# The first 512 columns of q and of k in one pass over x: both weight streams interleaved at the start of a decoder block

## The chip, the cores and the metric

The kernel runs on one core of one Trainium2 chip. The metric is the device time of one execution in microseconds (us), median of several runs.

## What is computed

A decoder block for one sequence of 256 tokens with a model width of 2048, in float32:

```python
hn   = rms_norm(h, pre_mix_norm)
proj = hn @ w_in                      # 2048 -> 1024 (pool) + 1024 (q) + 1024 (k) + 1024 (v)
pool = causal_multiscale_pool(u_pool, pool_w, pool_scale)
q, k = apply_partial_rope(q, positions), apply_partial_rope(k, positions)
attn = differential_attention(q, k, v, lam)          # 8 heads, causal, 256 x 256
h    = h + rms_norm(concat([pool, rms_norm(attn)]) @ w_out, post_mix_norm)
hn   = rms_norm(h, pre_ffn_norm)
h    = h + rms_norm((silu(hn @ w_gate) * (hn @ w_up)) @ w_down, post_ffn_norm)   # 5632 wide
```

The change concerns the very first products: `hn @ w_in` for the first 512 columns of q and the first 512 columns of k.

## The kernel before

**Products.** Every float32 product is made of three TensorE (PE) matmuls in a reduced float type: the operands are split into a high part (a rounded copy, made by ScalarE, ACT) and a low part (the rest, made by VectorE, DVE), and high x high, low x high and high x low are added up in PSUM. `mm_a` (lines 132 to 137) issues these three for one of the 16 slices of 128 rows of the contraction (a "k" of x below) and one of two blocks `t` of 128 tokens; 512 columns of weights stream through each matmul. So one k of x with 512 columns takes 2 x 3 = 6 matmuls, and 512 columns of output over all 16 k take 96.

**Weights.** They come from HBM in pieces of 128 partitions x 1024 elements (512 KB), that is two k of 512 columns, into a ring of `RAW = 6` raw tiles. `ring_parts` gives the split tiles: a ring of `RING = 3` pairs (`whi`, `wlo`). A raw tile is free for the next load when both halves of its split are done; a split tile is free when the last matmul on it is done. All loads but two are issued by SyncE's queue (SP), in the order of the program.

**The first product.** The first 512 columns of q are computed by a loop written out by hand (lines 269 to 293), because x itself arrives at the same time. Each x slice comes transposed (`xT`), is scaled by the norm's gain and split by `x_in` (lines 253 to 255: one ACT and one DVE instruction per k). For the first four k, weights and x come in single-k pieces (256 KB and 128 KB); from then on x comes four k at a time (512 KB) and weights in 512 KB pieces. The two results accumulate in the PSUM banks `ps0`.

**What follows.** After this loop stand the loads of positions, of constants and of x itself once more (2 MB, for the norm's statistics: `load_after` holds them behind the latest weight load), the squares and sums of x (line 308, ACT), the reciprocal root, and the sines and cosines. Then a loop over two groups `g` of four heads computes q, k and v with 512 columns each: `gemm_a` with the weights' ring, then `heads_in` (scale by the norm's factor `rq` or `r1`, rotate, transpose on PE), then the heads' attention (`head`), whose scores use the PSUM tile `sc` (two banks), the pooling branch and `heads_out`. For `g == 0`, q is what the first loop left in `ps0`, and k is a `gemm_a` of its own (line 514).

**Order.** Each engine executes its own instructions in a fixed order. That order is chosen when the program is built: a scheduler runs a simulated timeline and may put a later instruction ahead of an earlier one of the same engine, save where a dependence or `issue_after` forbids it. On the chip an engine then waits at whatever instruction stands next.

Of the kernel before, what the change touches and what calls it, by code (L numbers as in the profile page):

```python
# [8 lines left out]
F32 = mybir.dt.float32  # L9
F32R = mybir.dt.float32r  # L10
I32 = mybir.dt.int32
AF = mybir.ActivationFunctionType
ALU = mybir.AluOpType
AX = mybir.AxisListType

P = 128
S = 256
D = 2048
NKD = D // P
# [26 lines left out]
def block_kernel(ctx: ExitStack, tc: tile.TileContext, x, xT, pos, cols, rows, lamv, invf, invcnt,  # L46
                 w_in, w_u, w_pool, w_out, w_g0, w_u0, w_gu, w_down, out):
    nc = tc.nc
    mm, act, dve, pool, sync = nc.tensor, nc.scalar, nc.vector, nc.gpsimd, nc.sync
# [10 lines left out]
    def nm(s):  # L60
        uid[0] += 1
        return f"{s}_{uid[0]}"
# [4 lines left out]
    def bank():  # L67
        return psum.tile([P, 512], F32, tag="mm", name=nm("mm"), bufs=4)

    def bank2():  # L70
        return psum.tile([P, 512], F32, tag="tr", name=nm("tr"), bufs=2)


    latest = [None]

    def raw_tile(half=0):
        return ring.tile([P, 1024], F32, tag="raw", name=nm("raw"), bufs=RAW)
# [3 lines left out]
    def load(src, half):  # L81
        raw = raw_of[0](half)
        latest[0] = sync.dma_start(raw, src[:, half * 1024:(half + 1) * 1024]).ins
        return raw
# [6 lines left out]
    def ring_parts():  # L91
        return (ring.tile([P, 1024], F32R, tag=f"w{z}", name=nm(f"w{z}"), bufs=RING) for z in ("hi", "lo"))
# [18 lines left out]
    def a_steps(srcs, order=None, held=range(0), parts=None):  # L111

        i = 0
        for s in order or range(len(srcs)):
            raws = [load(srcs[s], half) for half in range(2)]
            for half in range(2):
                by = parts(i) if i in held else ()
                if by != "halves":
                    hi, lo = split(raws[half], *by)
                for j in range(2):  # L120
                    c = slice(j * 512, (j + 1) * 512)
                    if by == "halves":
                        w = split(raws[half][:, c], lambda: (half_tile("wh"), half_tile("wl")))
                    else:
                        w = hi[:, c], lo[:, c]
                    yield i, 4 * s + 2 * half + j, *w
                    i += 1
# [4 lines left out]
    def mm_a(ps, a, t, k, wh, wl, first, last):  # L132

        with tc.issue_after(behind[0]) if behind[0] is not None else nullcontext():
            mm.matmul(ps[t][:, :], lhsT=a[0](k, t), rhs=wh, start=first, stop=False)  # L135
            mm.matmul(ps[t][:, :], lhsT=a[1](k, t), rhs=wh, start=False, stop=False)  # L136
            last_mm[0] = mm.matmul(ps[t][:, :], lhsT=a[0](k, t), rhs=wl, start=False, stop=last).ins  # L137
# [3 lines left out]
    def gemm_a(srcs, a, nk, order=None, before=lambda i: None):  # L141
        ps = [bank(), bank()]
        for i, k, wh, wl in a_steps(srcs, order):
            before(i)
            for t in range(2):
                mm_a(ps, a, t, k, wh, wl, i == 0, i == nk - 1)
        return ps
# [85 lines left out]
    psum_sc = p_att.enter_context(tc.tile_pool(name="psum_sc", bufs=1, space=bass.MemoryType.PSUM))  # L233
    ap_ = p_att.enter_context(tc.tile_pool(name="ap", bufs=1))
# [16 lines left out]
    vtag = lambda name: ap_.tile([P, 1024], F32, tag="v", name=nm(name), bufs=2)  # L251

    def x_in(k, xr):
        act.activation(xh_k(k), xr, AF.Copy, scale=g1(k))
        dve.scalar_tensor_tensor(xl_k(k), xr, g1(k), xh_k(k).bitcast(F32), ALU.mult, ALU.subtract)
# [10 lines left out]
    a_x = (lambda k, t: xh_k(k)[:, t * P:(t + 1) * P], lambda k, t: xl_k(k)[:, t * P:(t + 1) * P])  # L266


    ps0 = [bank(), bank()]
    for i in range(4):  # L270
        xr = ap_.tile([P, 4, S], F32, tag="qk", name=nm("xr"), bufs=2) if i < 2 else vtag("xr").rearrange("p (a b) -> p a b", b=S)
        if i > 0:
            sync.dma_start(xr, xT[:, 4 * i:4 * i + 4, :])
        raws = [load(w_in[0, i], half) if i > 0 else raw_tile() for half in range(2)]
        for half in range(2):
            hi, lo = ring_parts()
            raw = raws[half]
            if i > 0:
                act.activation(hi, raw, AF.Copy)  # L279
            for j in range(2):  # L280
                k = 4 * i + 2 * half + j
                c = slice(j * 512, (j + 1) * 512)
                if i == 0:
                    (act if k == 0 else sync).dma_start(xr[:, k:k + 1, :], xT[:, k:k + 1, :])
                    latest[0] = sync.dma_start(raw[:, c], w_in[0, 0][:, half * 1024 + j * 512:half * 1024 + (j + 1) * 512]).ins
                x_in(k, xr[:, k - 4 * i, :])
                if i == 0:
                    act.activation(hi[:, c], raw[:, c], AF.Copy)
                if i == 0 or j == 0:
                    d = c if i == 0 else slice(0, 1024)  # L290
                    dve.tensor_tensor(lo[:, d], raw[:, d], hi[:, d].bitcast(F32), ALU.subtract)
                for t in range(2):
                    mm_a(ps0, a_x, t, k, hi[:, c], lo[:, c], k == 0, k == NKD - 1)


    post_t = tiny.tile([P, 2], I32, tag="pos", name="post", bufs=1)
# [67 lines left out]
    def heads_in(ps, scale, what, g):  # L364
        n = ap_.tile([P, 2, 512], F32, tag="qk", name=nm(what), bufs=2)
        for t in range(2):
            act.activation(n[:, t, :], ps[t][:, :], AF.Copy, scale=scale[:, t:t + 1])
        v = n.rearrange("p t (h d) -> p t h d", d=64)
        r16 = v[:, :, :, 0:16]
        shape = [P, 2, 8, 16]  # L370
        ra = ap_.tile(shape, F32, tag="ra", name=nm("ra"), bufs=1)
        rb = ap_.tile(shape, F32, tag="rb", name=nm("rb"), bufs=1)
        for t in range(2):
            cb = cos2[:, t].rearrange("p a b -> p (a b)")[:, None, :].to_broadcast([P, 8, 16])
            sb = sin2[:, t].rearrange("p a b -> p (a b)")[:, None, :].to_broadcast([P, 8, 16])
            dve.tensor_tensor(ra[:, t], r16[:, t], cb, ALU.mult)
            dve.tensor_tensor(rb[:, t], r16[:, t], sb, ALU.mult)
        dve.tensor_tensor(v[:, :, :, 0:8], ra[:, :, :, 0:8], rb[:, :, :, 8:16], ALU.subtract)
        dve.tensor_tensor(v[:, :, :, 8:16], ra[:, :, :, 8:16], rb[:, :, :, 0:8], ALU.add)
        res = []  # L380
        for hp in range(2):
            tr = bank2()
            for j in range(2):
                for t in range(2):
                    mm.transpose(tr[:, j * S + t * P: j * S + (t + 1) * P], n[:, t, (2 * hp + j) * P:(2 * hp + j + 1) * P], ident)
            o = mid.tile([P, 2, S], F32, tag="qkT", name=nm(what + "T"), bufs=8)
            act.activation(o.rearrange("p a b -> p (a b)"), tr[:, :], AF.Copy)
            res.append(o)
        return res
# [121 lines left out]
    for g in range(2):  # L511
        ps = ps0 if g == 0 else gemm_a([w_in[3 * g, i] for i in range(4)], a_x, NKD)
        qT += heads_in(ps, rq, "q", g)
        ps = gemm_a([w_in[3 * g + 1, i] for i in range(4)], a_x, NKD)
        kT += heads_in(ps, r1, "k", g)
        if g == 1:
            pool_mix(1)
        ps = gemm_a([w_in[3 * g + 2, i] for i in range(4)], a_x, NKD)
        for t in range(2):
            act.activation(vt[t][:, g * 512:(g + 1) * 512], ps[t][:, :], AF.Copy, scale=r1[:, t:t + 1])  # L520
        for h in range(4 * g, 4 * g + 4):
            head(h)
        for i in (3 - 2 * g, 2 - 2 * g):
            pool_u(i)
        heads_out(g)
# [132 lines left out]
    ps = gemm_a([w_u0[i] for i in range(4)], a_h, NKD, None, lambda i: h_sums(h_at[i]) if i in h_at else None)  # L658
# [84 lines left out]
    for c in range(1, NF // 4):  # L743
        m = {1: bank(), 2: bank(), 3: bank(), 4: bank(), 5: None, 6: bank2(), 7: psum_m.tile([P, 512], F32, tag="m7", name=nm("m7"), bufs=1), 8: bank2()}
# [165 lines left out]
```

## Time and profile before

| | |
|---|---|
| median of 3 runs | 1042.12 us (1040.69 to 1042.84) |
| the profiled execution | 1042.59 us, of which the profile's span is 1040.8 us |
| granted TensorE clock, mean | 0.997 |
| PE busy | 1018.6 us (98% of the span), 4787 matmuls |
| DVE busy | 733.4 us (70%) |
| ACT busy | 538.8 us (52%) |
| HBM read | 198.37 MB, 195 GB/s over the span |

A row of the profile's timeline reads: start, duration (both in us, from the span's start), engine, source line, operation, output<-inputs, shapes, count of merged instructions; in brackets, how long the engine sat idle before it and what ended that. `SPq` and `ACTq` are the instruction queues of SyncE and ScalarE that issue transfers. `PEld` is the load of a matmul's stationary operand. A matmul's row shows a duration of some 0.39 us, but matmuls overlap: the pitch is the distance from one start to the next.

### The profile page before, as it was taken

Reading aid. Unit: us, or ns where it says so; the run is one execution under the profiler, and the core shown is the slowest. Engines: PE = TensorE matmul, PEld = TensorE weight load, DVE = VectorE, ACT = ScalarE, POOL = GpSimd, SP = SyncE. Lnnn points to the kernel's source line nnn. Section 1 sums busy time; section 2 is a strip of 40 time slices with the busy share of each in tenths; the row PEclk is TensorE's granted clock in tenths of the full one; section 3 lists DMA queues with packets and bytes.
Section 4 is the critical chain, followed back from the end, with each engine's and each line's share of the span. In section 5 each row is a group of like instructions: output and inputs, shape, how many; then the busy total and the mean of one; then the engine's idle time right before and its main releaser. Section 6 shows DMA issues by size and latency. Waiting matters only on the chain.

```text
span 1040.8 us, 12565 instructions
## 1 busy us (share of the span) xinstructions
PE 1018.6 (98%) x4787; PEld 839.4 (81%) x4787; DVE 733.4 (70%) x847; ACT 538.8 (52%) x643; POOL 34.6 (3%) x57
## 2 busy tenths in 40 slices
PE   8999999999999999999999999999999999999996
PEld 5788888988877788888878878878888888888884
DVE  6648755875677978889798887888877664454444
ACT  6746545664547655454554545545555653343431
POOL 0003200210030000000000000000000000000000
PEclk9999999999999999999999999999999999999998
DMA  8853555456754556555655556645565575556542
GB/s 321 293 182 122 178 185 166 156 168 220 245 198 158 175 207 207 180 181 207 212 191 186 177 191 211 209 167 183 199 211 202 206 286 193 194 192 212 195 169 81
DMA packets 57517, 203.39 MB, mean 195 GB/s; under 512 B 6896, under 2 KB 7792, under 8 KB 56688
## 3 DMA queue, kind: packets, MB, share of 16 engines
q1 hardware_dynamic: 57168, 202.44, 56.8%
q8 instruction: 37, 0.61, 0.2%
q14 instruction: 24, 0.20, 0.1%
q10 hardware_dynamic: 288, 0.15, 0.0%
HBM read 198.37 MB, written 4.19 MB: 195 GB/s over the span
## 4 chain that ended last, share of the span: by engine, by line
PE 85%; DMA 6%; DVE 6%; issue 1%; SPq 1%; ACT 1%; DVEq 0%; ACTq 0%
PE mm L137 15%; PE mm L136 15%; PE mm L135 15%; PE mm L757 8%; PE mm L755 7%; PE mm L756 7%; DMA raw<-in_w_gu 4%; PE tr L757 2%; PE tr L756 2%; PE tr L755 2%; DVE wl L695 2%; PE mm L173 2%; PE mm L175 2%; PE mm L174 1%; PE m L755 1%; DVE xn L563 1%
## 5 line engine op out<-in xcount | busy, mean ns | idle before, releaser
L100 DVE TENSOR_TENSOR wl<-raw,wh 128x1024 fp32r<-128x1024 f32 x88 | 104.7, 1222 | 106.9 <-ACT wh L99 106.9
L100 DVE TENSOR_TENSOR wlo<-raw,whi 128x1024 fp32r<-128x1024 f32 x97 | 119.2, 1230 | 70.3 <-ACT whi L99 64.0
L99 ACT ACTIVATE wh<-raw 128x1024 fp32r<-128x1024 f32 x88 | 89.3, 1052 | 122.0 <-PE mm L136 117.3
L99 ACT ACTIVATE whi<-raw 128x1024 fp32r<-128x1024 f32 x97 | 102.1, 1057 | 78.0 <-PE mm L136 60.7
L136 PE MATMUL mm<-wh,gl 128*128 128x512 f32 x352 | 137.1, 390 | 0.0
L695 DVE TENSOR_TENSOR wl<-raw,wh 128x2048 fp32r<-128x2048 f32 x50 | 114.4, 2287 | 31.2 <-ACT wh L702 31.2
L135 PE MATMUL mm<-wh,gh 128*128 128x512 f32 x352 | 134.8, 389 | 0.0
L137 PE MATMUL mm<-wl,gh 128*128 128x512 f32 x352 | 130.7, 389 | 0.0
L755 PE MATMUL mm<-wh,h 128*128 128x512 f32 x330 | 128.6, 390 | 0.0
L756 PE MATMUL mm<-wh,h 128*128 128x512 f32 x330 | 128.6, 390 | 0.0
L757 PE MATMUL mm<-wl,h 128*128 128x512 f32 x330 | 115.6, 394 | 3.8 <-DVE wl L695 3.8
L702 ACT ACTIVATE wh<-raw 128x2048 fp32r<-128x2048 f32 x50 | 95.5, 1910 | 44.7 <-PE tr L756 39.8
L702 ACT ACTIVATE wh<-T 128x2048 fp32r<-128x2048 f32 x30 | 57.3, 1911 | 60.4 <-DVE T L706 55.4
L695 DVE TENSOR_TENSOR wl<-T,wh 128x2048 fp32r<-128x2048 f32 x30 | 68.6, 2287 | 23.1 <-ACT wh L702 23.1
L135 PE MATMUL mm<-whi,x 128*128 128x512 f32 x192 | 75.1, 395 | 3.5 <-ACT whi L279 2.7
L137 PEld LDWEIGHTS mm<-wl,gh 128*128 128x128 f32 x352 | 66.1, 188 | 13.7
L136 PEld LDWEIGHTS mm<-wh,gl 128*128 128x128 f32 x352 | 66.0, 188 | 13.8
L757 PEld LDWEIGHTS mm<-wl,h 128*128 128x128 f32 x330 | 61.9, 188 | 18.7 <-DVE wl L695 6.1
L135 PEld LDWEIGHTS mm<-wh,gh 128*128 128x128 f32 x352 | 66.0, 188 | 13.5
L136 PE MATMUL mm<-whi,x 128*128 128x512 f32 x192 | 74.6, 391 | 0.0
L756 PEld LDWEIGHTS mm<-wh,h 128*128 128x128 f32 x330 | 61.9, 188 | 13.0
L755 PEld LDWEIGHTS mm<-wh,h 128*128 128x128 f32 x330 | 62.0, 188 | 12.6
(243 smaller groups left out, 1910.6 us busy)
## 6 DMA issues: line engine op xcount, KB each, us to landing
raw<-in_w_gu SPq DMA_DIRECT2D x160, 512.0 KB, 4.5
raw<-in_w_down SPq DMA_DIRECT2D x88, 512.0 KB, 4.1
raw<-in_w_in SPq DMA_DIRECT2D x46, 512.0 KB, 3.7
raw<-in_w_out SPq DMA_DIRECT2D x32, 512.0 KB, 4.0
raw<-in_w_u SPq DMA_DIRECT2D x24, 512.0 KB, 3.6
raw<-in_w_g SPq DMA_DIRECT2D x8, 512.0 KB, 5.9
xn<-in_x SPq DMA_DIRECT2D x2, 1024.0 KB, 9.1
gain<-in_rows SPq DMA_DIRECT2D x8, 256.0 KB, 4.9
```

Source lines behind the costliest of these rows:

```text
L99: last_split[0] = act.activation(hi, raw, AF.Copy).ins
L100: (by or dve).tensor_tensor(lo, raw, hi.bitcast(F32), ALU.subtract)
L135: mm.matmul(ps[t][:, :], lhsT=a[0](k, t), rhs=wh, start=first, stop=False)
L136: mm.matmul(ps[t][:, :], lhsT=a[1](k, t), rhs=wh, start=False, stop=False)
L137: last_mm[0] = mm.matmul(ps[t][:, :], lhsT=a[0](k, t), rhs=wl, start=False, stop=last).ins
L173: mm.matmul(o, lhsT=wh, rhs=xh, start=st, stop=False)
L175: mm.matmul(o, lhsT=wl, rhs=xh, start=False, stop=sp)
L695: last_low[0] = dve.tensor_tensor(res, x, hi.bitcast(F32), ALU.subtract).ins
L702: act.activation(res, x, AF.Copy)
L755: mm.matmul(o, lhsT=a[0], rhs=wh, start=first, stop=False)
L756: mm.matmul(o, lhsT=a[1], rhs=wh, start=False, stop=False)
L757: mm.matmul(o, lhsT=a[0], rhs=wl, start=False, stop=left[i] == 0)
```

## The change

The first loop now goes over the 16 k of x and, for each, does q's 512 columns and k's 512 columns one after the other: 12 matmuls for each k of x where there were 6. q accumulates in `ps0` as before, k in `ps1`, which is the first use of the PSUM tile `sc` that the heads' scores use later. Only the first two k come in single-k pieces; x of k = 2 and 3 comes as one 256 KB piece, the rest of x four k at a time; from k = 2 on weights come in 512 KB pieces, q's and k's in turn. The loads are issued in the order x, q's weights, k's weights. The `gemm_a` for k of the first group is dropped; the loads of positions and constants and of x for the statistics now stand behind the loads of both weight streams, since `latest` is then the last of them.

```diff
     ps0 = [bank(), bank()]
-    for i in range(4):
-        xr = ap_.tile([P, 4, S], F32, tag="qk", name=nm("xr"), bufs=2) if i < 2 else vtag("xr").rearrange("p (a b) -> p a b", b=S)
-        if i > 0:
-            sync.dma_start(xr, xT[:, 4 * i:4 * i + 4, :])
-        raws = [load(w_in[0, i], half) if i > 0 else raw_tile() for half in range(2)]
-        for half in range(2):
-            hi, lo = ring_parts()
-            raw = raws[half]
-            if i > 0:
-                act.activation(hi, raw, AF.Copy)
-            for j in range(2):
-                k = 4 * i + 2 * half + j
-                c = slice(j * 512, (j + 1) * 512)
-                if i == 0:
-                    (act if k == 0 else sync).dma_start(xr[:, k:k + 1, :], xT[:, k:k + 1, :])
-                    latest[0] = sync.dma_start(raw[:, c], w_in[0, 0][:, half * 1024 + j * 512:half * 1024 + (j + 1) * 512]).ins
-                x_in(k, xr[:, k - 4 * i, :])
-                if i == 0:
-                    act.activation(hi[:, c], raw[:, c], AF.Copy)
-                if i == 0 or j == 0:
-                    d = c if i == 0 else slice(0, 1024)
-                    dve.tensor_tensor(lo[:, d], raw[:, d], hi[:, d].bitcast(F32), ALU.subtract)
-                for t in range(2):
-                    mm_a(ps0, a_x, t, k, hi[:, c], lo[:, c], k == 0, k == NKD - 1)
+    sc0 = psum_sc.tile([P, 2, 512], F32, tag="sc", name="sc0", bufs=1)
+    ps1 = [sc0[:, t] for t in range(2)]
+    xrs = [ap_.tile([P, 4, S], F32, tag="qk", name=nm("xr"), bufs=2) if i < 2 else vtag("xr").rearrange("p (a b) -> p a b", b=S) for i in range(4)]
+    raws = {}
+    for k in range(NKD):
+        n = 1 if k < 2 else 2
+        i, j = k // 4, k % 4
+        if k < 2 or k % 4 == 0 or k == 2:
+            x_z = slice(j, j + (1 if k < 2 else 2 if k == 2 else 4))
+            (act if k == 0 else sync).dma_start(xrs[i][:, x_z, :], xT[:, k:k + x_z.stop - x_z.start, :])
+        if j % 2 == 0:
+            raws = [(raw_tile(), *ring_parts()) for _ in range(2)]
+        for m in range(2):
+            raw, hi, lo = raws[m]
+            c = slice(j % 2 * 512, (j % 2 + n) * 512)
+            if n == 1 or j % 2 == 0:
+                latest[0] = sync.dma_start(raw[:, c], w_in[m, i][:, j * 512:(j + n) * 512]).ins
+        x_in(k, xrs[i][:, j, :])
+        for m in range(2):
+            raw, hi, lo = raws[m]
+            if n == 1 or j % 2 == 0:
+                c = slice(j % 2 * 512, (j % 2 + n) * 512)
+                act.activation(hi[:, c], raw[:, c], AF.Copy)
+                dve.tensor_tensor(lo[:, c], raw[:, c], hi[:, c].bitcast(F32), ALU.subtract)
+            c = slice(j % 2 * 512, (j % 2 + 1) * 512)
+            for t in range(2):
+                mm_a((ps0, ps1)[m], a_x, t, k, hi[:, c], lo[:, c], k == 0, k == NKD - 1)
...
-        ps = gemm_a([w_in[3 * g + 1, i] for i in range(4)], a_x, NKD)
+        ps = ps1 if g == 0 else gemm_a([w_in[3 * g + 1, i] for i in range(4)], a_x, NKD)
         kT += heads_in(ps, r1, "k", g)
```

## The prediction

> **What bounds the kernel now.** First the page: the span's share of each engine and the chain of work that ended last.
>
> ```profile
> span 1040.8 us, 12565 instructions
> ...
> PE 1018.6 (98%) x4787; PEld 839.4 (81%) x4787; DVE 733.4 (70%) x847; ACT 538.8 (52%) x643; POOL 34.6 (3%) x57
> ...
> PE 85%; DMA 6%; DVE 6%; issue 1%; SPq 1%; ACT 1%; DVEq 0%; ACTq 0%
> ```
>
> PE is the bound, and the change neither adds nor removes a matmul. A gain can come only from PE's idle time, 1040.8 - 1018.6 = 22.2 us in all. PE's waits in the first 130 us, apart from the very start, name two:
>
> ```profile
> PE mm L135 <- ACT whi L279: 2.7, 1, 2.7
> ...
> PE mm L135 <- ACT whi L99: 0.8, 1, 0.8
> ```
>
> One lies in the rewritten stage (line 279), one at the seam behind it (line 99); PE's timeline gives places and sizes.
>
> ```profile
> 5.24 1.15 PE L135 MATMUL mm<-whi,x 128*128 128x512 f32 x2
> ...
> 7.16 0.62 PE L135 MATMUL mm<-whi,x 128*128 128x512 f32 x2
> 7.61 0.61 PE L136 MATMUL mm<-whi,x 128*128 128x512 f32 x2
> ...
> 10.78 0.61 PE L137 MATMUL mm<-wlo,x 128*128 128x512 f32 x2
> 14.11 0.50 PE L135 MATMUL mm<-whi,x 128*128 128x512 f32 x1 [2.71 <-ACT whi L279]
> ...
> 15.93 0.40 PE L135 MATMUL mm<-whi,x 128*128 128x512 f32 x1
> ...
> 30.70 0.39 PE L137 MATMUL mm<-wlo,x 128*128 128x512 f32 x1
> 31.86 0.50 PE L135 MATMUL mm<-whi,x 128*128 128x512 f32 x1 [0.77 <-ACT whi L99]
> ...
> 33.68 0.40 PE L135 MATMUL mm<-whi,x 128*128 128x512 f32 x1
> ```
>
> The undisturbed pitch is (7.61 - 7.16) / 2 = 0.227 us. The first 24 matmuls (four k of q) run from 5.24 to about 11.24; the first six need 1.92 us instead of 1.36, since the low part of x comes late. The next matmul starts at 14.11: 2.87 us lost. The six starts from 14.11 to 15.93 take 1.82 instead of 1.36 (the low part of the weights comes late): 0.46. At the seam from q to k, 30.70 to 31.86 is 0.93 too much, and 31.86 to 33.68 again 0.46: together 1.39.
>
> What ended these waits is seen on ACT and DVE, and behind them in the transfers:
>
> ```profile
> 8.24 0.63 ACT L288 ACTIVATE whi<-raw 128x512 fp32r<-128x512 f32 x1
> 11.40 1.71 ACT L254 ACTIVATE x<-xr,colt 128x256 fp32r<-128x256 f32 x4 [2.53 <-DMA xr<-in_xT]
> 13.01 2.10 ACT L279 ACTIVATE whi<-raw 128x1024 fp32r<-128x1024 f32 x2
> ...
> 26.33 1.91 ACT L308 ACTIVATE junk<-xn 128x2048 bf16<-128x2048 f32 x1 [2.54 <-DMA xn<-in_x]
> ...
> 30.76 1.04 ACT L99 ACTIVATE whi<-raw 128x1024 fp32r<-128x1024 f32 x1
> 31.82 1.28 ACT L197 ACT_TABLE_LOAD   x1
> ...
> 14.09 2.36 DVE L291 TENSOR_TENSOR wlo<-raw,whi 128x1024 fp32r<-128x1024 f32 x2 [0.46 <-ACT whi L279]
> ```
>
> At 11.40 the second piece of x lands; ACT then makes four high parts of x (1.71) and only then the first high part of weights (1.05), at whose end PE starts. At the seam, 2 MB of x for the statistics stand between q's and k's weights; ACT does their squares first and k's first split at 30.76. Both losses are transfers' arrivals:
>
> ```profile
> 5.00:10.00 5.00, 5.00 (x21) 3.96 (x20) 3.85 (x8) 3.27 (x7) 0.00 (x0) 1.00 0.94 302
> 10.00:15.00 5.00, 2.29 (x11) 1.49 (x9) 2.60 (x5) 3.60 (x6) 0.00 (x0) 1.00 1.01 396
> ```
>
> (Busy time of PE, PEld, DVE, ACT, POOL, then granted clock, DMA share, GB/s.) From 10 us on the transfers are saturated, at 396 GB/s (DMA share 1.01).
>
> **The change, part by part.**
>
> *Demand.* Before, two k of q take 256 KB of x and 512 KB of weights for 12 matmuls (2.73 us): 288 GB/s. Now one k takes 128 + 512 KB for 12 matmuls: 240 GB/s. Both are below 396; what counts is the order of arrival.
>
> *The start.* x of k = 0 is issued by ACT as before, but SP's second transfer is now k's 256 KB of weights instead of 128 KB of x, so x may land later by up to 128 KB, 0.35 us at some 380 GB/s (between the 302 and the 396 of the first two windows, nearer to the second). PE then starts between 5.24 and 5.59. I take 0.3, and it is covered: the 24 matmuls (now two k) then end at 11.5, before the next weights can be split.
>
> *The next weights (largest term).* Ahead of the first 512 KB piece there stand, before, four weight pieces of 256 KB and four x pieces of 128 KB; now four of 256 KB, two of 128 KB and one of 256 KB: 1536 KB both times. So q's weights for k = 2, 3 take the place of x's second piece, landing at 11.40. Earliest: the last small weights were split from 8.24 without a wait, and a 512 KB piece later takes 1.28 us (between x's second and fourth piece lie six such pieces, and that fourth one lands at 8.78 + 10.29 = 19.07: 7.67 / 6), so 9.5. Latest: one piece later, 12.7. I take 11.4, since the queue is filled the same way. x of k = 2 and 3 has landed by then, so ACT's split follows at once: 11.4 + 1.05 = 12.45, PE restarts at 12.5. Before it did at 14.11. Gain 1.6; the ends give 2.5 (no stall at all: 14.11 - 11.57) and 0.3.
>
> ```profile
> 8.78 10.29 DMA xr<-in_xT
> 19.09 9.74 DMA xn<-in_x
> ```
>
> *The late low part.* DVE's subtraction takes 1.18 to 1.22 and starts when ACT ends; four matmuls (0.91) stand before its first use. Same shape as at 14.11: 0.46 lost again, difference 0 (ends 0 and +0.46, should the bank order give it eight matmuls to hide in).
>
> *The weights after that.* By 1.28 us per 512 KB: k's for k = 2, 3 at 12.7, x at 14.0, the next pair at 15.2 and 16.5, where PE wants them at 12.5 + 5.46 + 0.46 = 18.4. From there transfers run ahead. Stall 0.
>
> *The seam.* The 2 MB of x now queue behind all of q's and k's weights, and what comes next on PE is v, wanted after 168 more matmuls from 12.5: 12.5 + 0.46 + 38.1 = 51. The last weight load waits for a raw tile until 30.2 (worked out below). Unhurried loads take 3.7 us to land:
>
> ```profile
> raw<-in_w_in SPq DMA_DIRECT2D x46, 512.0 KB, 3.7
> ```
>
> So that one lands at 33.9, x behind it at 36.5 and 39.0 (2.56 us per MB), then v's first weights. All are there before 51, so the 1.39 goes. Cover: 12 us of matmuls; without it the cost is again about 1.4. What is late next is no transfer: v's weights, 512 KB per 12 matmuls (2.73 us), are 192 GB/s, half of the 396.
>
> *Split tiles.* Here the change costs something. With three split tiles and two streams, the k half of a pair reuses the tile of the q half one pair earlier: free after 18 of that pair's 24 matmuls, wanted 12 matmuls (2.73 us) later, its low part 4 later still (3.64). Split takes 1.05 + 1.22, so 1.2 us of slack; before, a tile was free 24 matmuls (5.46 us) ahead. The same count gives the last load: tile of the fifth pair (12.96 + 2 x 5.46 + 4.1 is 28, split until 30.2). In that phase ACT also does two squares of 1.91 and table loads of 1.28. One of them falling into the 2.7 us at its worst costs 1.91 - 1.2 = 0.7 of PE. Ends: 0 and 2 x 0.7 + 3 x 0.1 = 1.7; I take 0, since the chance that a 1.9 us piece covers the one moment per 5.46 us with over 1.2 left is (1.9 - 1.2) / 5.46, about 1 in 8.
>
> *heads_in* for q moves from k's product to v's: both then share v's 21.8 us (96 matmuls). The rows for it:
>
> ```profile
> L367 ACT ACTIVATE k<-mm,r 128x512 f32<-128x512 f32 x2 | 1.4, 684 | 0.9 <-PE mm L137 0.9
> ...
> 52.07 1.09 ACT L387 ACTIVATE qT<-tr 128x512 f32<-128x512 f32 x2 [1.83 <-PE tr L385]
> ...
> 45.96 0.49 DVE L376 TENSOR_TENSOR ra<-q,cos 128x128 f32<-128x128 f32 x2
> 46.62 0.28 DVE L378 TENSOR_TENSOR q<-ra,rb 128x128 f32<-128x128 f32 x1
> ```
>
> ACT: 8 splits of 1.05, 4 copies of 0.68, two pairs of 1.09, 13.3 us. DVE: 8 x 1.2 and, for each of q and k, 2 x 0.49 + 2 x 0.28, 12.9 us. Both fit. PE's transposes only move. The scores' PSUM tile is wanted after v, long after k's copy out of it. Cost 0; uncovered, it would delay v's splits by a copy, 0.7.
>
> Sum: 1.6 + 0 + 1.39 = 3.0. The profiled execution took 1042.59 (span 1040.8 and 1.8 around), so 1039.6; the median of the runs lies 0.47 lower, hence **1039.1**.
>
> **The rivals.**
>
> *A faster second pair (0.17).* q's second weights land near 9.5. For: the transfer share was 0.94 in 5 to 10, not 1.0. Against: the same 1536 KB ahead. Gain 2.5 + 1.39 = 3.9, up to 4.3 with the low part hidden: 1038.2 to 1037.8.
>
> *Slack eaten (0.30): no measurable change.* ACT waits at the square for x, as it did at 26.33 (2.54), with a split queued behind. Behind x's second MB at 39.0 a square and 0.2 of read-out (to 41.1) and the split (42.2) meet a want of 40.3 (the seventh pair's q half, 12.96 + 5 x 5.46) to 41.7 (its k half): 0.5 to 1.9 lost, and the table loads take their 0.1 each. Gain 0.8 to 2.2: 1039.9 to 1041.3, taken as up to 2.1. For: slack falls from 5.46 to 2.73. Against: x now comes with little queued ahead.
>
> *Statistics too late (0.09): slower.* One mechanism: x's second half lands late, and ACT's order has both squares ahead of the splits of the seventh pair; PE's wait is then landing + 2.1 + 1.05 - 40.3. At 39.0 that is 1.9; over 42.3 it exceeds 3.0 + 2.1 and the kernel is slower by over 0.2%. At 43 it gives 1042.1 + 2.9 = 1045.0. Against: x took 9.74 from issue with a full queue; issued at 32 and lying for 9.74 again it would land at 41.8, which is not yet enough.
>
> *The clock (0.03).* PE's idle stretch before the second pair grows and PE restarts slowly. The 9 warm-up matmuls of the same shape take 4.02 / 9 = 0.45 each:
>
> ```profile
> 1.45 4.02 PE L249 MATMUL tr<-warm 128*128 128x512 bf16 x9 [1.45 <-DVE warm L245]
> ```
>
> Should a restart be as slow for as long as those (9 x 0.22 = 2.0 lost) after weights 2.5 us later than forecast, the gain is 3.0 - 4.5: 1043.6. Against: the 2.71 idle at 14.11 left the granted clock at 1.00, and the pitch behind it at 0.23. The Trainium skill, "TensorE: Matmul & The Clock Gate", Part 1 (the HAM clock gate), states that an idle window of about 3.4 us halves the clock; the trace agrees so far as 2.71 did not do it. By that rule the weights would have to land past 13.9.
>
> **How the numbers follow.** 0.2% is 2.1 us, about what a measurement here can tell from no change. Likeliest (0.41): 3.0 saved, 1039.1, own range 1038.5 to 1040.0. With the faster second pair (0.17) that is 0.58 faster. Slack eaten (0.30) and the clock (0.03) are within 0.2%: 0.33. Slower 0.09. The range runs from 1037.4 (4.3 gained, and 0.4 for the spread of the runs) to 1042.4; the slower case and the edge of the clock's lie outside.
>
> **What would show it.** Right: PE's second restart at 12 to 13 us with 24 matmuls before it, waiting for ACT's `whi` and this for a weight transfer, not x; no gap of PE between 18 and 51; squares of x on ACT between 35 and 41. Wrong: PE waiting on `whi` or `wlo` between 30 and 51, ACT idle for `xn` just ahead of a split, or the matmuls that turn `r1` into a row (line 214) waiting on DVE.

## The result and the profile after

The changed kernel takes 1058.24 us (1053.71 to 1062.06, 4 runs), the one before in the same runs 1042.44: ratio 1.0154, interval 1.0132 to 1.0175. It is slower by 1.5%, where 1039.1 was forecast. The profiled execution took 1060.05 us. Its page begins:

```profile
span 1058.2 us, 12574 instructions
...
PE 1022.4 (97%) x4787; PEld 840.4 (79%) x4787; DVE 732.7 (69%) x847; ACT 538.3 (51%) x643; POOL 36.4 (3%) x57
...
PE 77%; DVE 9%; DMA 7%; issue 4%; ACT 2%; SPq 0%; DVEq 0%; ACTq 0%
```

The work is the same (4787 matmuls, 847 and 643 instructions on DVE and ACT), the span is 17.4 us longer, and in the chain PE's share fell from 85% to 77%: PE waits for others more often. The next view is PE's waits, of the first 130 us (first fence) and of the whole kernel (second).

```profile
PE mm L135 <- ACT x L254: 0.9, 1, 0.9
PE mm L135 <- ACT whi L292: 0.3, 1, 0.3
```

```profile
PE mm L760 <- DVE wl L698: 5.6, 8, 1.3
PE mm L758 <- ACT rh L705: 5.5, 6, 1.6
PE m L758 <- ACT gT L679: 5.0, 9, 0.7
PE mm L758 <- ACT wh L705: 3.9, 4, 1.0
```

Where the change was made, the waits of 2.7 and 0.8 us are gone. The new ones, 20.0 us against 4.3 (`PE mm L757 <- DVE wl L695: 3.8, 4, 1.2` and 0.5 for `rh`), stand in the FFN's loop over ten chunks of gate and up weights, whose code the change does not touch (its lines are 3 higher after). To see when the time goes, take the start of the n-th matmul in both traces (counted from 0, the 9 warm-ups included; up to each number in the table the same kinds of matmuls have been done, as often) and subtract:

| matmul | where | before | after | difference |
|---|---|---|---|---|
| 33 | second pair of the first stage | 14.11 | 12.45 | -1.66 |
| 129 | behind the seam | 37.80 | 34.70 | -3.10 |
| 716 | behind the first four heads | 141.74 | 136.85 | -4.89 |
| 1770 | ahead of the FFN loop | 346.44 | 342.02 | -4.42 |
| 4200 | behind it | 897.27 | 914.69 | +17.42 |
| 4786 | the last | 1030.10 | 1047.52 | +17.42 |

The start gained 4.9 us, more than forecast, and the FFN loop lost 21.8. Of these, 15.7 are PE's listed waits (20.0 - 4.3) and some 3.4 are two stretches of 3.41 us at half clock in the loop (last section); the other 2.7 are not attributed. The windows show in what form the time is lost (busy us of PE, PEld, DVE, ACT, POOL; clock; DMA share; GB/s), one chunk of the loop in each: one of before, then four of after:

```profile
401.00:444.00 43.00, 42.97 (x193) 34.93 (x192) 36.48 (x31) 23.41 (x19) 0.00 (x0) 1.00 0.56 194
```

```profile
401.00:450.00 49.00, 44.73 (x197) 35.36 (x195) 38.79 (x33) 23.69 (x19) 0.00 (x0) 1.00 0.49 172
450.00:492.00 42.00, 41.50 (x185) 34.36 (x186) 33.95 (x29) 22.00 (x16) 0.00 (x0) 1.00 0.58 201
492.00:542.00 50.00, 46.49 (x199) 36.73 (x197) 40.38 (x34) 22.36 (x16) 0.00 (x0) 0.97 0.48 168
542.00:585.00 43.00, 42.31 (x191) 34.83 (x189) 33.20 (x29) 22.15 (x16) 0.00 (x0) 1.00 0.57 196
```

Before, every chunk takes 43 to 44 us; after, they alternate between some 49 and 42. ACT's timeline at the end of a chunk shows what differs, first before, then after:

```profile
439.47 1.92 ACT L702 ACTIVATE wh<-T 128x2048 fp32r<-128x2048 f32 x1 [4.95 <-DVE T L706]
441.29 1.32 ACT L795 ACTIVATE sg<-sg,rstd 128x512 f32<-128x512 f32 x2
442.59 1.92 ACT L702 ACTIVATE wh<-raw 128x2048 fp32r<-128x2048 f32 x1
444.41 1.47 ACT L702 ACTIVATE rh<-raw 128x1536 fp32r<-128x1536 f32 x1
```

```profile
433.99 1.92 ACT L705 ACTIVATE wh<-T 128x2048 fp32r<-128x2048 f32 x1 [4.27 <-PE tr L759]
443.08 1.48 ACT L705 ACTIVATE rh<-raw 128x1536 fp32r<-128x1536 f32 x1 [7.17 <-DMA raw<-in_w_gu]
444.47 0.71 ACT L798 ACTIVATE sg<-sg,rstd 128x512 f32<-128x512 f32 x1
445.08 1.90 ACT L705 ACTIVATE wh<-raw 128x2048 fp32r<-128x2048 f32 x1
446.88 0.71 ACT L798 ACTIVATE sg<-sg,rstd 128x512 f32<-128x512 f32 x1
```

The instructions are the same, their order isn't: the next chunk's split (`rh`) now stands ahead of the silus (`sg`), and as its load has not landed, ACT sits idle for 7.17 us with the silus behind it (DVE had written the second one's input by 440.54, and it began at 446.88). The order of the FFN loop on PE, ACT and DVE was written anew at build time; SP's order of the loads, and every engine's order between the attention and the loop, are as before. The transfers show the rest. SP issues a load when its raw tile is free:

```profile
SPq L693 <- DVE wl L698: 330.2, 48, 14.5
```

Before, the same row read `SPq L690 <- DVE wl L695: 306.0, 48, 8.6` over the loop: the longest wait for a tile grew from 8.6 to 14.5 us, so some loads go out later and come late.

### The profile page after: what moved, and what is told of

It reads as the page before. It is cut to its first block, busy times and chain, and to the rows that moved or that the text cites. A ratio compares the mean times of both kernels' runs of the same rounds, so it can differ in the third digit from the quotient of the medians.

```text
span 1058.2 us, 12574 instructions
## 1 busy us (share of the span) xinstructions
PE 1022.4 (97%) x4787; PEld 840.4 (79%) x4787; DVE 732.7 (69%) x847; ACT 538.3 (51%) x643; POOL 36.4 (3%) x57
## 4 chain that ended last, share of the span: by engine, by line
PE 77%; DVE 9%; DMA 7%; issue 4%; ACT 2%; SPq 0%; DVEq 0%; ACTq 0%
PE mm L137 15%; PE mm L136 14%; PE mm L135 14%; DMA raw<-in_w_gu 6%; PE mm L760 6%; PE mm L758 6%; PE mm L759 6%; DVE wl L698 3%; DVE T L709 2%; PE tr L758 2%; PE tr L759 2%; PE tr L760 2%; PE mm L173 2%; PE mm L174 1%; PE mm L175 1%
## 5 line engine op out<-in xcount | busy, mean ns | idle before, releaser
L100 DVE TENSOR_TENSOR wlo<-raw,whi 128x1024 fp32r<-128x1024 f32 x89 | 110.4, 1241 | 61.4 <-ACT whi L99 56.4
L99 ACT ACTIVATE whi<-raw 128x1024 fp32r<-128x1024 f32 x89 | 93.7, 1056 | 64.2 <-PE mm L136 49.5
L759 PEld LDWEIGHTS mm<-wh,h 128*128 128x128 f32 x330 | 62.5, 189 | 12.9
L705 ACT ACTIVATE rh<-raw 128x1536 fp32r<-128x1536 f32 x30 | 44.6, 1487 | 54.7 <-DMA raw<-in_w_gu 54.5
L135 PE MATMUL mm<-whi,x 128*128 128x512 f32 x160 | 62.5, 393 | 1.2 <-ACT x L254 0.9
```

The source lines that it names most:

```text
L99: last_split[0] = act.activation(hi, raw, AF.Copy).ins
L100: (by or dve).tensor_tensor(lo, raw, hi.bitcast(F32), ALU.subtract)
L705: act.activation(res, x, AF.Copy)
L759: mm.matmul(o, lhsT=a[1], rhs=wh, start=False, stop=False)
```

## The experiments

All times are medians beside runs of the kernel before on the same chip (1041.76, 1042.06 and 1040.80 in the three groups). "Loop" is the time from matmul 1770 to 4200: 550.8 before, 572.7 in the changed kernel.

**Is it the order?** Two kernels cross start and FFN order. Marking the position where the loop's code begins, the traced instructions of each engine are chained in the order of the other kernel, without any wait between them:

```diff
+    ffn_from = len(nc.cur_bb.bb.instructions)
     ready = prepare(1, 0)
...
+    traced = list(nc.cur_bb.bb.instructions)[ffn_from:]
+    for kind, order in FFN_ORDER.items():
...
+        for a, b in zip(order, order[1:]):
+            tc.add_manual_dep(mine[b], mine[a].name, mybir.DependencyInfo(mybir.DependencyClass.NoSync, mybir.DependencyReason.DATA), reason="order")
     p_ft.close()
```

`FFN_ORDER` holds 1910 positions for PE, 162 for ACT, 304 for DVE.

> The changed kernel, with the instructions of the FFN loop (gate and up products) on PE, ACT and DVE held in the order that they have in the kernel before; nothing else differs from the changed kernel. In the traces the changed kernel reaches the output projection's end 4.4 us earlier (PE's first transpose at line 589 starts at 297.9 instead of 302.4), and then loses some 22 us in the FFN loop, whose order differs. Theory 'order' (the build's scheduler wrote another order for the FFN loop, and that alone costs): 1042.4 - 4.4 = 1038.0, range 1037.2 to 1039.0. Rival 'chip' (the new start leaves something that slows the FFN stage on the chip, such as transfers or the clock, and the order is not the cause): 1054 to 1062, as the changed kernel.

Measured: 1036.52 us (1034.46 to 1038.13), ratio 0.9947, interval 0.9933 to 0.9961, which is 0.7 us below the theory's range and far from the rival's. Loop 548.3; the start is ahead by 5.6 at matmul 1770.

> The kernel before, with the instructions of the FFN loop held in the order that they have in the changed kernel; its first 350 us are those of the kernel before. Theory 'order': 1042.4 + 22 = 1064, range 1056 to 1067. Rival 'chip': 1042.4, within 1.

Measured: 1062.49 us (1061.89 to 1065.27), ratio 1.0203, interval 1.0186 to 1.0220. At matmul 1770 the trace is 0.7 us ahead of before's, at 4200 19.3 behind; the loop takes 570.9. PE's waits in the loop are nearly those of the changed kernel:

```profile
PE mm L764 <- DVE wl L701: 5.8, 7, 1.3
PE mm L762 <- ACT rh L708: 5.5, 6, 1.5
PE m L762 <- ACT gT L682: 5.0, 9, 0.7
PE mm L762 <- ACT wh L708: 4.0, 4, 1.0
```

So the change of the start is good by some 5 us with the old order (1041.76 - 1036.52), and the new order alone costs some 20, whichever start stands ahead of it (1062.49 - 1041.76 with the old one, 1058.24 - 1036.52 with the new one). The order is the cause of the loss; what in it costs is the question of the runs below.

**What flips the order?** Three small edits of the start, with nothing held. First one more warm-up matmul, which makes the build write exactly before's order of the loop:

```diff
-WARM = 9
+WARM = 10
```

> The changed kernel with WARM = 10 instead of 9 (one more warm-up matmul ahead of the first product, in time in which PE waits for x anyway). Built so, the FFN loop comes out in the order of the kernel before, without any order being held by hand. Theory 'order': 1038.0, range 1037.2 to 1039.0. Rival 'chip': 1054 to 1062.

Measured: 1037.55 us (1035.30 to 1037.98), ratio 0.9954, interval 0.9941 to 0.9967. Loop 550.1. One matmul of 0.45 us, in the first microseconds, is worth 20 us.

Second, the kernel before, with k of the first group accumulated in the two banks of `sc` and nothing else:

```diff
-    def gemm_a(srcs, a, nk, order=None, before=lambda i: None):
-        ps = [bank(), bank()]
+    def gemm_a(srcs, a, nk, order=None, before=lambda i: None, ps=None):
+        ps = ps or [bank(), bank()]
...
+    sc_t = psum_sc.tile([P, 2, 512], F32, tag="sc", name="sc0", bufs=1)
+    sc0 = [sc_t[:, t] for t in range(2)]
...
-        ps = gemm_a([w_in[3 * g + 1, i] for i in range(4)], a_x, NKD)
+        ps = gemm_a([w_in[3 * g + 1, i] for i in range(4)], a_x, NKD, ps=sc0 if g == 0 else None)
```

> The kernel before with one part of the change alone: k's product of the first group adds up in the two banks of the scores' tile (sc) instead of two of the four mm banks; loads, loops and the start as before. Built so, the FFN loop comes out in a third order. Theory 'order': the first 300 us within 0.5 us of the kernel before, and the FFN loop takes another time than before, more likely longer (this order alternates from chunk to chunk as the changed kernel's does): 1045 to 1064. Rival 'chip': 1042.4 within 1.

Measured: 1067.52 us (1062.01 to 1073.62), ratio 1.0248, interval 1.0219 to 1.0278. At matmul 1770 it is 1.1 us behind before (a stretch at half clock in the first stage, told below, costs more than that), the loop takes 575.2, in yet another order, and the time is above the theory's range. The banks themselves cost nothing that shows ahead of the loop.

Third, five warm-up matmuls, which gives one more order:

```diff
-WARM = 9
+WARM = 5
```

> The changed kernel with 5 instead of 9 warm-up matmuls at the very start and nothing held: the scheduler then writes a third order of the FFN loop, neither that of before nor that of the changed kernel. Theory: the order of before is the exception and most others lose some 20 us: 1052 to 1070. Rival: only the order of the changed kernel is bad and a third one is as good as before's: 1035 to 1040.

Measured: 1052.94 us (1051.50 to 1056.31), ratio 1.0120, interval 1.0094 to 1.0146; loop 565.7. The order of before is the exception among those tried.

**What did the start gain, and from what?** The seam alone: k's product issued right behind q's loop, so that x for the statistics stands behind k's weights; no interleaving; the FFN order held as before.

```diff
+    ps1 = gemm_a([w_in[1, i] for i in range(4)], a_x, NKD)
     post_t = tiny.tile([P, 2], I32, tag="pos", name="post", bufs=1)
...
-        ps = gemm_a([w_in[3 * g + 1, i] for i in range(4)], a_x, NKD)
+        ps = ps1 if g == 0 else gemm_a([w_in[3 * g + 1, i] for i in range(4)], a_x, NKD)
```

> Half of the change alone: q and k are not interleaved; k's product is merely issued right behind q's loop, so that the loads of positions, constants and x for the statistics stand behind k's weights. The order of the FFN loop on PE, ACT and DVE is held as in the kernel before. Theory: the 1.39 us at the seam from q to k go, the 2.87 + 0.46 us at the second pair stay, and PE's order in the heads' stage, which in the new kernel had fewer changes between score matmuls (64 rows) and others and gained 1.8 us, changes here too: 1.4 to 3.2 us below before, against 5.2 for the whole change with the old FFN order. Rival 1: nearly all of the start's gain came from the interleaving, since x for the statistics is as late here as before: 0 to 0.5 below before. Rival 2: the gain in the heads' stage belongs to the interleaving alone: 1.4 below before and PE's heads' stage as before.

Measured: 1038.43 us (1036.76 to 1039.72), ratio 0.9964, interval 0.9949 to 0.9978: 3.6 us below before, just over the theory's 3.2, and neither rival fits. Against before, PE is 0.71 ahead at matmul 93, 2.14 at 129 and 3.94 at 716. The step from 93 to 129, 1.43 us, is the seam; in the changed kernel the same step is 3.10 - 1.66 = 1.44. The step from 129 to 716 is 1.80 here and 1.79 (4.89 - 3.10) there, so it belongs to neither the interleaving nor the seam's stall: in the heads' stage PE's order is new too. Before's timeline has score matmuls (64 rows) and transposes of `e` in turn, after's has them apart:

```profile
89.24 0.49 PE L405 MATMUL sc<-kT,qT 64*128 64x128 f32 x4
89.66 0.33 PE L431 MATMUL tr<-ident,e 128*128 128x128 f32 x1
89.92 0.70 PE L408 MATMUL sc<-kT,qT 64*128 64x256 f32 x2
90.55 0.44 PE L431 MATMUL tr<-ident,e 128*128 128x128 f32 x2
90.91 0.70 PE L408 MATMUL sc<-kT,qT 64*128 64x256 f32 x2
91.54 0.39 PE L173 MATMUL mm<-x,whi 128*128 128x256 f32 x1
```

```profile
85.51 0.49 PE L408 MATMUL sc<-kT,qT 64*128 64x128 f32 x4
85.83 0.60 PE L411 MATMUL sc<-kT,qT 64*128 64x256 f32 x4
86.36 0.38 PE L173 MATMUL mm<-x,whi 128*128 128x256 f32 x1
```

Eight score matmuls and three transposes take 2.30 us before; the eight take 0.85 us after, and the three transposes stand between other matmuls later. Part of the 1.8 us seems to lie in such places (14 changes between score matmuls and others up to matmul 600, against 8): no run changes this order alone, and the rest is open.

**Which engine's order costs?** The changed kernel with two engines' FFN order held as before, and one as in the changed kernel (the same edit with other lists).

> The changed kernel, with the FFN loop's order on PE and DVE held as in the kernel before and only ACT's as in the changed one (next chunk's split of a raw tile between the two silus, the split of sh ahead of the copy s1). Theory: ACT's order carries the loss, because a split that waits for a load stands ahead of the second silu and what follows it: 15 to 25 us over the run with all three orders as before (1036.5), so 1051 to 1061. Rival: DVE's order carries it: 1036 to 1039 here. Second rival: it takes both: 1040 to 1050 in this run and in the next one.

> The changed kernel, with the FFN loop's order on PE and ACT held as in the kernel before and only DVE's as in the changed one (low part of a load ahead of the gate's arithmetic). Theory: ACT's order carries the loss: 1036 to 1039 here. Rival: DVE's order carries it: 1051 to 1061. Second rival: it takes both: 1040 to 1050 here and in the run before.

Measured: 1100.03 us (ratio 1.0558, interval 1.0531 to 1.0585) with ACT's order new, 1123.86 (ratio 1.0786, 1.0764 to 1.0808) with DVE's. All three theories fell: each mixture is far worse than both pure orders (1036.5 and 1058). With DVE's alone, PE waits for the low parts:

```profile
PE mm L767 <- DVE wl L704: 42.8, 18, 3.7
PE mm L767 <- DVE rl L704: 13.4, 4, 3.4
```

The orders of the engines fit one another: neither ACT's nor DVE's carries the loss by itself. PE's new order with the two old ones was not run.

**One pair by hand.** Two orders fixed in every chunk, the rest left to the build: the split of `sh` behind the copy `s1`, the next chunk's first split behind the second silu.

```diff
+                tc.add_manual_dep(sh_split, copied.name, ...)
...
+        if c < NF // 4 - 1:
+            tc.add_manual_dep(highs[-2], silu.name, ...)
```

> The changed kernel with two orders fixed by hand in each chunk of the FFN loop: the split of sh behind the copy s1, and the next chunk's first split of a raw tile behind the second silu. The scheduler orders the rest itself, and the order that comes out is neither of the two known ones. Theory: the next chunk's split between the silus is what costs; with it behind them the time is within 3 us of the run with the whole old order, 1036 to 1040. Rival: the loss lies in other parts of the order (DVE's low parts ahead of the gate's arithmetic, as in the changed kernel): over 1045.

Measured: 1080.42 us (1078.69 to 1085.09), ratio 1.0381, interval 1.0358 to 1.0404. The theory fell: moving the split that looks so bad in the timeline above is not enough. But the build then orders the rest in another way, on every engine, and PE waits 17.3 us for `rh`, so this run leaves open what the split costs by itself.

**Is it the loads?** The new order held fixed, with a little SBUF freed as control, and then with a fourth raw tile; the same with before's order.

```diff
-CMB = 8
+CMB = 6
...
-        res = fp.tile([P, 512], F32, tag="gg", name=nm("gg"), bufs=3)
+        res = fp.tile([P, 512], F32, tag="gg", name=nm("gg"), bufs=2)
...
-        raw = part("raw", 4, F32, 3)
+        raw = part("raw", 4, F32, 4)
```

> Control for the next run. The changed kernel with its own order of the FFN loop held fixed on PE, ACT and DVE, and a little SBUF freed (six instead of eight tiles for the sums, two instead of three for the gated products). Both theories: as the changed kernel, 1053 to 1062.

> The run before with one edit: four instead of three tiles for the loaded weights of the FFN loop, same instruction order on every engine, so that the 1 MB loads can be issued one block earlier. Theory: the new order costs because raw tiles come free late and in bunches and ACT then waits for the load with the silus and the gate's copies queued behind (54.5 us of ACT's waits for w_gu and 25.4 of DVE's): with the spare tile PE's extra 15.7 us of waits in the loop mostly go, 1040 to 1046. Rival: the engines wait for one another whatever the loads do (ACT behind PE's transposes and DVE's sums, PE behind the low parts): within 3 us of the control.

> The changed kernel with the FFN order of the kernel before held, and four instead of three raw tiles (and the same SBUF freed as in the control). Both theories: the old order has about 2 us of PE waits for the low parts left in the loop, so 1034 to 1037, at most 2 below the run with three tiles (1036.5).

Measured: control 1062.48 us (1058.75 to 1064.36; 0.5 above its range), loop 571.0; new order with four tiles 1046.87 (1044.36 to 1047.87), ratio 1.0052, interval 1.0034 to 1.0070, loop 559.2; old order with four tiles 1031.75 (1030.19 to 1033.01), ratio 0.9910, interval 0.9894 to 0.9926, loop 544.3. PE's waits in the control, and with four tiles:

```profile
PE mm L767 <- DVE wl L704: 7.7, 6, 1.5
PE m L765 <- ACT gT L685: 5.0, 9, 0.7
PE mm L765 <- ACT wh L711: 4.0, 4, 1.0
PE mm L765 <- ACT rh L711: 4.0, 4, 1.6
```

```profile
PE mm L767 <- DVE wl L704: 7.2, 5, 1.4
PE m L765 <- ACT gT L685: 5.0, 9, 0.7
```

At the place shown above, ACT no longer waits for a load:

```profile
435.04 1.48 ACT L711 ACTIVATE rh<-raw 128x1536 fp32r<-128x1536 f32 x1
```

The spare tile takes away all 8.0 us of waits for `rh` and `wh`, and 11.8 us of the loop. So late loads are part of the cost, as the theory had it, though 1046.87 is just above its range. The tile helps the old order too, by 4.0 us of the loop (548.3 to 544.3) where at most 2 were expected; no run has the old order with the freed SBUF and three tiles. Like for like, the new order costs 22.7 us with three tiles (571.0 - 548.3) and 15.0 with four (559.2 - 544.3): a third of its cost goes with the spare tile, and two thirds stay. Of the 15.0, PE's listed waits are 7.2 + 5.0 and a stretch at half clock (below) 1.7; which part of the order makes these waits is open. The old order with four tiles has no PE wait left in the loop and is the fastest kernel here.

## Why the prediction was wrong

- *The start.* PE's first real matmul came at 6.34, not between 5.24 and 5.59: the price was three times its bound, but covered as said (the 24 matmuls end at 11.96, the restart is later). The nine other profiles of this start (one with five and one with ten warm-up matmuls) have 5.98 to 6.15. That the order of the loads makes this price isn't shown: the kernel with the seam alone, whose first loads stand as before, has 6.21.
- *The next weights.* Right in mechanism: ACT's split began at 11.33 (forecast 11.4), PE restarted at 12.45 (12.5), gain 1.66 (1.6). That the numbers meet within 0.1 is luck: in the nine other profiles of this start PE comes to the second pair at 11.66 to 13.82, and in the three of before's start at 12.85 to 14.11.

```profile
11.33 1.06 ACT L292 ACTIVATE whi<-raw 128x1024 fp32r<-128x1024 f32 x1 [1.80 <-DMA raw<-in_w_in]
...
12.45 0.50 PE L135 MATMUL mm<-whi,x 128*128 128x512 f32 x1 [0.33 <-ACT whi L292]
...
14.28 0.39 PE L135 MATMUL mm<-whi,x 128*128 128x512 f32 x1
```

- *The late low part.* Right: 12.45 to 14.28 is 1.83 us for six starts, 1.82 before.
- *The weights after that, the seam, the split tiles.* Right: no PE wait between 15 and 130 us; the seam gave 1.44 (1.39). The slack of a split tile is 3.64 - 2.27 = 1.37 by the prediction's own figures, not 1.2, and DVE's 12.9 us under *heads_in* are 12.7; nothing hangs on either.
- *x for the statistics* was forecast at 36.5 and 39.0. ACT's first square waited until 39.77:

```profile
39.77 1.91 ACT L311 ACTIVATE junk<-xn 128x2048 bf16<-128x2048 f32 x1 [1.32 <-DMA xn<-in_x]
41.59 0.19 ACT L311 ACTIVATION_READ_ACCUMULATOR junk<-xn 128x1 f32 x1
41.68 1.05 ACT L292 ACTIVATE whi<-raw 128x1024 fp32r<-128x1024 f32 x1
42.63 1.90 ACT L311 ACTIVATE junk<-xn 128x2048 bf16<-128x2048 f32 x1
```

The rivals "slack eaten" and "too late" needed both squares ahead of the splits; here a split stands between them. ACT idle for `xn` just ahead of a split was named as a sign of being wrong. ACT did sit idle for 1.32 us, ahead of a square with a split behind it, and PE did not wait.
- *heads_in, cost 0.* Too simple: the heads' stage gained 1.8 us by another order on PE.
- *The sum.* 3.0 was forecast, 4.89 came by matmul 716, and 5.2 us net with the old FFN order (1041.76 - 1036.52). The step that failed is none of the listed ones: it is the silent one that every stage behind the heads stays as it is, a term put at nothing without a reason. The front part of the document says that the order is chosen at build time by a simulated timeline; neither the parts of the change nor the rivals drew the conclusion that an earlier start re-times every later choice. In its place the runs showed a new order of the FFN loop: it cost 21.8 us, in a stage 300 us behind the change, and no rival named it.
- *The clock.* Given 0.03 as a stretch behind the start's idle time. The changed kernel has half-clock stretches, but in the FFN loop. At the start the clock matters in another way: in five of the nine other profiles of this start the first matmuls run at a pitch of 0.43 us instead of 0.23 until the clock rises at 9.75 to 10.76 us (5.64 in the changed kernel's profile above), and PE then comes to the second pair at 13.30 or later without any wait. In the three profiles of before's start it rises by 7.27. The first product now stands 0.5 to 0.9 us behind the nine warm-up matmuls, where it followed within 0.12; whether this gap keeps the clock down isn't shown.

## What to carry to other kernels

Where a scheduler fixes each engine's order at build time, an edit has a term for every stage behind it: compare the order of the untouched stages in both builds before looking at a trace, and hold an order that was found good, else one matmul of 0.45 us can move a time by 20. Test whether an order matters by crossing it with the old code, all engines together: a single engine's order taken alone (1100 and 1124 us) says nothing. A loop that loses time to the order may be short of slack, and some can be bought: a fourth raw tile gave back 11.8 of the 22.7 us that a bad order cost and made the good one faster by 4.0.

## What the runs showed of the clock

The granted clock fell to half for stretches of 3.41 us (twice 6.83) in the middle of several kernels, after idle times much shorter than that. In the changed kernel, PE's waits ahead of one such stretch were 0.96 and 0.97 us. The windows before and in it (PE's busy time first, the clock third from the end):

```profile
534.71:538.12 3.41, 1.73 (x6) 1.15 (x7) 3.41 (x5) 3.41 (x4) 0.00 (x0) 1.00 0.00 0
538.12:541.53 3.41, 3.41 (x9) 2.58 (x9) 3.41 (x4) 0.75 (x2) 0.00 (x0) 0.50 0.00 0
```

Nine matmuls pass; before's window from 14.80 to 18.20 has 15. The starts of such stretches lie on a grid of 3.413 us that runs on from the first change of the clock. Over the 14 profiles here, 36 windows of the grid ahead of the kernel's end had PE busy for less than 1.46 us, by its modelled ends, and behind each of them the clock was halved for the next; so it was behind 4 of the 9 with 1.47 to 1.73, and behind none of the others that ran at full speed. Where the grid lies decides. The kernel with k in `sc` has the first stage of before and an idle time of 2.47 us ahead of its second pair, all of it in one window; before's 2.71 us are cut in two by the grid:

```profile
11.38:14.79 3.41, 0.95 (x4) 0.67 (x4) 2.65 (x5) 3.40 (x6) 0.00 (x0) 1.00 1.02 418
14.79:18.21 3.42, 3.42 (x9) 2.48 (x8) 3.42 (x7) 2.73 (x6) 0.00 (x0) 0.50 1.03 414
```

```profile
9.59:13.01 3.42, 1.81 (x8) 1.15 (x7) 1.08 (x4) 1.61 (x4) 0.00 (x0) 1.00 1.01 393
13.01:16.42 3.41, 2.25 (x9) 1.56 (x10) 2.95 (x5) 3.28 (x6) 0.00 (x0) 1.00 1.03 407
```

The Trainium skill, "TensorE: Matmul & The Clock Gate", Part 1 (the HAM clock gate), has a free-running window of about 3.4 us, and the grid agrees; it has the clock halved after an idle window of that length, and there the measurement decides: a window with PE busy for under 1.46 of its 3.41 us was enough in every case here. The reading of 2.71 us in the prediction (idle, yet no lower clock) was luck of the grid.
